# Two norms' affine moved into the MLPs, score bias by DMA, and low weight halves on VectorE through the attentions

## The chip, the cores and the metric

The kernel runs on one core of one Trainium2 chip. A core has TensorE (PE), VectorE (DVE), ScalarE (ACT), GpSimd (POOL) and SyncE (SP), each with its own in-order queue, and DMA queues beside them. The metric is the device time of one execution in microseconds; before, it is 1722.39 us, the median of three runs (1721.23 to 1723.97).

## The reference

Two layers of a diffusion transformer of width 1024 run over 512 latent tokens and 128 prompt tokens. Each layer is an attention mixer and a squared-ReLU MLP, each with a modulated input, a gated residual and a layer norm behind it. Layer 0 has differential attention, layer 1 attention over a two-dimensional neighbourhood with a learned bias.

```python
def layer_norm(x, g, b): return (x - mean(x)) * rsqrt(var(x) + eps) * g + b
def modulate(x, shift, scale): return x * (1 + scale) + shift
def sq_relu_mlp(h, w1, w2): return square(relu(h @ w1)) @ w2

for i in range(DEPTH):                         # DEPTH = 2; the same for xp (prompt) and xs (latent)
    y = mixer[i](modulate(xs, ms[0], ms[1]), caches[i], params[i])
    xs = layer_norm(ALPHA * xs + ms[2] * y, ln_g[i, 0], ln_b[i, 0])
    y = sq_relu_mlp(modulate(xs, ms[3], ms[4]), w_mlp1[i], w_mlp2[i])
    xs = layer_norm(ALPHA * xs + ms[5] * y, ln_g[i, 1], ln_b[i, 1])

# layer 1, latent tokens: window scores get a bias, context scores none
ln = einsum('bchd,bicjhd->bhcij', q, k_window) * scale + bias   # bias = rpb[rel. row, rel. col]
p = softmax(concat([ln, q @ ck * scale]))
```

## The kernel before

**Tokens and precision.** The 640 tokens are five tiles of 128 (`NTT`); the activations that a product reads are kept transposed, 1024 features by 640 tokens, as a high part and a low part (`hhi`, `hlo`, or `uhi`, `ulo` inside the MLP). Weights are split in the same way, and each product is three matmuls (`mm3`, L117 to L121): high by high, high by low, low by high.

**Weights.** They stream through a ring of five groups of 128x1024 (`RING`). For each group `conv` (L188 to L199) has ScalarE copy the raw tile to its high part `wh` (L194), and two subtractions of 128x512, the "halves", make the low part `wl` (L196). `self.pool_lo` says how many of the two GpSimd makes; the others are VectorE's. The conversion of a group is issued when an old group has been used for the last time (`used`, `done`), so conversions come in bursts of three or four at the end of a chunk. `pool_lo` is 2 at the start, 1 in most of the attentions and in the MLPs, and 2 from the steps named "X" near the end of each attention, through its projection, up to the MLP.

**Order.** TensorE's order is written by hand: the strings `ORDER0`, `ORDER1` and `ORDER_LN` name steps which `Net.run` calls. On the other engines a scheduler sets the order of the queue. In the attentions, S is a score step, T its transposes, P the product with V, B the bias of a score step. Behind the last head come the projection (o, j), the gated residual (g), the transposes of the normalised rows (h), the first up-projections (f) and W, which closes.

**Norms after attention.** For each token tile `gated` multiplies the projection by the gate (`tmp`, L1167), adds it to X (L1169 or L1171), takes statistics (L1034), and `ln_pre` (L1036 to L1044) ends in one subtract-and-multiply of 128x1024 (`X`, L1044). `ln_h` transposes X (L1073), has ScalarE apply the next modulation (its coefficients `AB` are per feature), and splits the result into `hhi` and `hlo` (L127). The norm's own g and b reach X, which is the residual of the next part, by two GpSimd instructions of 128x1024 (L1084, L1085), issued by step W. Between the layers the same functions work in the order `ORDER_LN`; there the GpSimd affine is issued tile by tile, and X then goes to DRAM (`x1`).

**MLP.** `rest` runs four groups; each has two up chunks (`ff`, then `act`: Relu on ScalarE L1230, square on VectorE L1231, split into `uhi` and `ulo`) and two down passes of five token tiles (`nat`, then `add_gated_sb`, L1117 to L1121).

**Layer-1 scores.** For a pair of heads and a block of 128 queries `scores1` makes two 128x384 score tiles. `qk_rows` (L456 to L460) does a 128-row matmul for each head with the high part of Q, then for each head a matmul of 64 rows with its low part. `bias1` (L813) prepares the tile E on GpSimd from a column mask and a table of one head pair; E has six buffers, freed by the transposes (L884).

Of the kernel before, what the change touches and what calls it, by code (L numbers as in the profile page):

```python
# [18 lines left out]
P = 128  # L19
# [30 lines left out]
    g1 j02 j13 h0 g2 j03 j04 h1 j14 g3 g4 h2 f0 f2 h3 f3 h4 f1 W  # L50
# [10 lines left out]
    h4 f3 f2 W  # L61
# [4 lines left out]
class Net:  # L66
# [163 lines left out]
    def consts(self):  # L230
# [11 lines left out]
        self.sc = c.tile([P, KT, 32], F32, name="sc")  # L242
# [78 lines left out]
    def mod_affine(self, l, s, k=None):  # L321
# [6 lines left out]
        pl, ps = (l, 0) if s == 1 else (l - 1, 1)  # L328
        g = self.lnc[:, pl, ps, 0, :].unsqueeze(2).to_broadcast([P, KT, 2])
        b = self.lnc[:, pl, ps, 1, :].unsqueeze(2).to_broadcast([P, KT, 2])  # L330
# [123 lines left out]

    def qk_rows(self, out, Q, K, q, k):
        te = self.nc.tensor  # L456
        for x in range(2):
            te.matmul(out[x], Q[:, x, q], k(K[:, x]), start=True, stop=False)
        for x, r in enumerate(HALF):
            te.matmul(out[x], Q[r, 2, q], k(K[r, x]), start=False, stop=True)  # L460

# [215 lines left out]
    def layer0_attn(self, acc0):  # L677
        nc, a = self.nc, self.a
        with self.tc.tile_pool(name="at0", bufs=1) as pool:
            self.q0 = pool.tile([P, 4, NT], F32R, name="q0")  # L680
            self.Vs, self.QKs = {}, {}
            self.pool_lo = 1
# [45 lines left out]
            def swap():  # L728
                self.pool_lo = 2
# [8 lines left out]

            def ln():
                t = pool.tile([P, 2, D], F32, tag="aTh", name="lnt")  # L740
                for x, n in enumerate(("lng", "lnb")):
                    nc.gpsimd.dma_start(t[:, x, :], a[n][0, 0].partition_broadcast(P))
                return t[:, 0, :], t[:, 1, :]
# [47 lines left out]
    def qk1(self, pool, i, x, n, c):  # L791
        nc, h, (w, hf) = self.nc, self.h, divmod(x, 2)
        if i not in self.QKs:
            Q = pool.tile([P, 3, NT], F32R, tag="Q", name=self.nm("Q"), bufs=2)
            K = pool.tile([P, 2, 768], F32R, tag="K", name=self.nm("K"), bufs=2)
            self.QKs[i] = (Q, K)
            self.cached_k(pool, self.a["ck1T"][i], K[:, :, 256:384])
# [9 lines left out]
        if w == 0:  # L807
            for s, d, k in (((0, 448, 64), (64, 0, 256)), ((0, 256, 192), (192, 512, 128)))[hf]:
                c, src = slice(d, d + k), m[:, s : s + k]
                nc.scalar.activation(Q[:, 0:2, c], src.unsqueeze(1).to_broadcast([P, 2, k]), AF.Copy, scale=-0.125)  # L810
# [609 lines left out]
```

## Time and profile before

| | |
|---|---|
| median of three runs | 1722.39 us |
| the profiled execution | 1720.29 us, its span 1718.5 us |
| mean granted TensorE clock | 0.98 |
| TensorE busy | 1630.8 us |
| VectorE busy | 1130.0 us |
| ScalarE busy | 662.0 us |
| GpSimd busy | 594.6 us |

The stages by the trace: start 0 to 54 us; layer-0 attention 54 to 405; its projection and norm to 458; first MLP to 870; norm between the layers to 930; layer-1 attention to 1224; its projection and norm to 1280; second MLP to the end. Times of instructions and waits are those of the profiled execution. A granted clock of 1.00 is the higher of TensorE's two levels, 2.4 GHz; a stretch with a lower figure ran in part at the lower one. An engine's idle time matters only where the engine that sets the end waits for it.

### The profile page before, as it was taken

Reading aid. Unit: us, or ns where it says so; the run is one execution under the profiler, and the core shown is the slowest. Engines: PE = TensorE matmul, PEld = TensorE weight load, DVE = VectorE, ACT = ScalarE, POOL = GpSimd, SP = SyncE. Lnnn points to the kernel's source line nnn. Section 1 sums busy time; section 2 is a strip of 40 time slices with the busy share of each in tenths; the row PEclk is TensorE's granted clock in tenths of the full one; section 3 lists DMA queues with packets and bytes.
Section 4 is the critical chain, followed back from the end, with each engine's and each line's share of the span. In section 5 each row is a group of like instructions: output and inputs, shape, how many; then the busy total and the mean of one; then the engine's idle time right before and its main releaser. Section 6 shows DMA issues by size and latency. Waiting matters only on the chain.

```text
span 1718.5 us, 25925 instructions
## 1 busy us (share of the span) xinstructions
PE 1630.8 (95%) x10026; PEld 1461.4 (85%) x10026; DVE 1130.0 (66%) x2015; ACT 662.0 (39%) x1338; POOL 594.6 (35%) x457
## 2 busy tenths in 40 slices
PE   8999999898799999999998999999789999999997
PEld 5798998786798988988978889997689898898996
DVE  4788778865748789798466677778684333242338
ACT  2466545643521221312234556565263122131321
POOL 2111112124632246264257233433373223324322
PEclk9999999999899999999999999999999999999999
DMA  8442234332334445353323222233133121222221
GB/s 331 134 136 95 88 126 137 108 128 67 123 99 142 165 137 184 124 184 120 99 69 128 79 79 79 78 102 115 59 109 98 50 98 62 86 64 85 85 64 62
DMA packets 59086, 187.96 MB, mean 109 GB/s; under 512 B 7396, under 2 KB 14034, under 8 KB 57938
## 3 DMA queue, kind: packets, MB, share of 16 engines
q1 hardware_dynamic: 55890, 174.89, 30.8%
q0 software_dynamic: 3072, 11.40, 1.9%
q8 instruction: 79, 1.29, 0.3%
q14 instruction: 45, 0.37, 0.1%
HBM read 176.25 MB, written 7.40 MB: 107 GB/s over the span
## 4 chain that ended last, share of the span: by engine, by line
PE 72%; DVE 15%; issue 4%; POOL 4%; ACT 3%; DMA 2%; SPq 0%; DVEq 0%; POOLq 0%; ACTq 0%
PE M L119 14%; PE M L121 14%; PE M L120 14%; PE S L121 8%; PE S L119 7%; PE S L120 7%; DVE wl L196 4%; POOL wl L196 2%; DVE hlo L127 1%; DVE X L1044 1%; POOL X L1084 1%; PE M L259 1%; PE M L595 1%; PE M L884 1%; POOL X L1085 1%
## 5 line engine op out<-in xcount | busy, mean ns | idle before, releaser
L196 POOL TENSOR_TENSOR wl<-rw,wh 128x512 fp32r<-128x512 f32 x209 | 345.7, 1674 | 589.5 <-ACT wh L194 543.5
L194 ACT CAST wh<-rw 128x1024 fp32r<-128x1024 f32 x192 | 196.9, 1050 | 347.3 <-PE M L121 270.0
L121 PE MATMUL S<-hhi,wl 128*128 128x320 f32 (+1 forms) x944 | 293.7, 311 | 6.1 <-DVE wl L196 4.7
L119 PE MATMUL S<-hhi,wh 128*128 128x320 f32 (+1 forms) x944 | 292.8, 310 | 0.0
L120 PE MATMUL S<-hlo,wh 128*128 128x320 f32 (+1 forms) x944 | 292.1, 309 | 0.0
L119 PE MATMUL M<-wh,uhi 128*128 128x512 f32 x640 | 249.6, 390 | 1.0 <-ACT uhi L126 1.0
L121 PE MATMUL M<-wh,ulo 128*128 128x512 f32 x640 | 249.3, 389 | 0.3
L120 PE MATMUL M<-wl,uhi 128*128 128x512 f32 x640 | 249.2, 389 | 0.0
L196 DVE TENSOR_TENSOR wl<-rw,wh 128x512 fp32r<-128x512 f32 x175 | 208.8, 1213 | 52.2 <-ACT wh L194 50.9
L119 PE MATMUL M<-wh,hhi 128*128 128x256 f32 (+1 forms) x640 | 202.4, 316 | 9.4 <-DVE tmp L1167 8.4
L121 PE MATMUL M<-wh,hlo 128*128 128x256 f32 (+1 forms) x640 | 197.1, 308 | 4.0 <-DVE hlo L127 3.9
L120 PE MATMUL M<-wl,hhi 128*128 128x256 f32 (+1 forms) x640 | 196.9, 308 | 2.5 <-DVE wl L196 2.5
L121 PEld LDWEIGHTS S<-hhi,wl 128*128 128x128 f32 x944 | 179.1, 190 | 10.1 <-DVE wl L196 8.3
L120 PEld LDWEIGHTS S<-hlo,wh 128*128 128x128 f32 x944 | 179.3, 190 | 0.2
L119 PEld LDWEIGHTS S<-hhi,wh 128*128 128x128 f32 x944 | 179.3, 190 | 0.2
L293 DVE SCALAR_TENSOR_TENSOR jk<-wm,cb 128x1024 bf16<-128x1024 f32 x96 | 142.5, 1484 | 1.5
L119 PEld LDWEIGHTS M<-wh,uhi 128*128 128x128 f32 x640 | 120.1, 188 | 26.5 <-ACT uhi L126 1.9
L121 PEld LDWEIGHTS M<-wh,ulo 128*128 128x128 f32 x640 | 120.1, 188 | 26.2 <-DVE ulo L127 1.1
L120 PEld LDWEIGHTS M<-wl,uhi 128*128 128x128 f32 x640 | 120.1, 188 | 24.5
L119 PEld LDWEIGHTS M<-wh,hhi 128*128 128x128 f32 x640 | 124.9, 195 | 18.0 <-DVE tmp L1167 8.9
L1231 DVE SCALAR_TENSOR_TENSOR r<-S,r 128x640 f32<-128x640 f32 (+1 forms) x62 | 48.5, 782 | 138.0 <-ACT r L1230 137.9
L121 PEld LDWEIGHTS M<-wh,hlo 128*128 128x128 f32 x640 | 124.5, 195 | 12.3 <-DVE hlo L127 7.7
(280 smaller groups left out, 3059.2 us busy)
## 6 DMA issues: line engine op xcount, KB each, us to landing
rw<-in_w SPq DMA_DIRECT2D x192, 512.0 KB, 4.1
wm<-in_wmodT SPq DMA_DIRECT2D x48, 512.0 KB, 3.5
rw<-in_wmod SPq DMA_DIRECT2D x32, 512.0 KB, 4.5
wm<-in_wmod SPq DMA_DIRECT2D x8, 1024.0 KB, 10.2
gate<-gates POOLq DMA_DIRECT2D x6, 512.0 KB, 5.0
X<-in_xT SPq DMA_DIRECT2D x8, 320.0 KB, 10.4
X<-in_xn SPq DMA_DIRECT2D x5, 512.0 KB, 5.4
x<-X SPq DMA_DIRECT2D x5, 512.0 KB, 2.8
```

The costliest lines, as they stand in the source:

```text
L119: te.matmul(out, sh, mh, start=start, stop=False)
L120: te.matmul(out, sh, ml, start=False, stop=False)
L121: te.matmul(out, sl, mh, start=False, stop=stop)
L127: nc.vector.tensor_tensor(lo, src, hi, ALU.subtract)
L194: keep(nc.scalar.copy(hi, r))
L196: keep(eng.tensor_tensor(lo[:, k], r[:, k], hi[:, k], ALU.subtract))
L259: self.nc.tensor.matmul(acc[32 * j : 32 * j + 32, :256], self.sc[:, 4 * r + j, :], w[:, j, :], start=r == 0, stop=r == 1, tile_position=(0 ...
L293: op = nc.vector.scalar_tensor_tensor(jk, ws[t], 1.0, cb[:, x, :], ALU.mult, ALU.mult, accum_out=mc[:, t, x : x + 1])
L595: nc.tensor.transpose(t[:, P * (j - j0) : P * (j - j0) + P], E[:, P * j : P * j + P], self.idf)
L884: nc.tensor.transpose(t[:, P * y : P * y + P], pr["E", b][:, x, c : c + P], self.idf)
L1044: nc.vector.tensor_scalar(x, x, mv[:, 0:1], rs, ALU.subtract, ALU.mult)
L1231: nc.vector.scalar_tensor_tensor(rv, src, 0.0, rv, ALU.max, ALU.mult)
```

## The change

It has five parts.

- *Norm affine.* The norms after the attentions no longer apply g and b at step W, which goes. In `rest`, behind the first Relu of the second up chunk of group 0, ten GpSimd instructions (`affine`: multiply, add for each tile) do it; they read `lng` and `lnb` loaded a little earlier, and the second norm's pair is loaded after them.
- *Norm between the layers.* `ln_mid` takes the place of `ln_pre` there: two scalar_tensor_tensor instructions on VectorE, (x - mean) * g and x * rstd + b, and the store of X to `x1`. `mod_affine` no longer folds g and b into those coefficients.
- *Low halves.* `pool_lo` is 0 from the layer-0 attention up to the first down pass of the first MLP, and again from the last down pass of the first MLP to the first down pass of the second: both halves on VectorE. In between it is 1, as before.
- *Scores.* Q has four slots, its low part written for both heads like its high part; `qk` does full 128-row matmuls for both, so that the low part of Q now meets the low part of K too. The swap DMA of Q doubles from 160 to 320 KB.
- *Bias.* E is loaded ready-made, 128x768 in float32, by one DMA on GpSimd's queue for each of the 32 score steps; the mask, the head-pair tables and GpSimd's work on them go. The exponential's sign conventions follow.

```diff
@@ consts, layer0_attn, layer1_attn
-        self.sc = c.tile([P, KT, 32], F32, name="sc")
+        self.sc = pool.tile([P, KT, 32], F32, name="sc")
-            self.pool_lo = 1
+            self.pool_lo = 0
             def swap():
-                self.pool_lo = 2
             def early():
-                self.pool_lo = 2
-            self.pool_lo = 1
@@ mod_affine
-        pl, ps = (l, 0) if s == 1 else (l - 1, 1)
+        if s == 0:
+            nc.vector.tensor_scalar(AB[:, 0], sc, 1.0, None, ALU.add)
+            nc.vector.tensor_copy(AB[:, 1], sh)
+            return
@@ qk1
-            Q = pool.tile([P, 3, NT], F32R, tag="Q", name=self.nm("Q"), bufs=2)
+            Q = pool.tile([P, 4, NT], F32R, tag="Q", name=self.nm("Q"), bufs=2)
-                nc.vector.scalar_tensor_tensor(Q[:, 2, c], src, -0.125, Q[:, 0, c], ALU.mult, ALU.subtract)
+                nc.vector.scalar_tensor_tensor(Q[:, 2:4, c], two, 0.125, Q[:, 0:2, c], ALU.mult, ALU.subtract)
-                    nc.sync.dma_start(Q[HALF[1 - y], y, :].bitcast(F32), Q[r, y, :].bitcast(F32))
+                    nc.sync.dma_start(Q[HALF[1 - y], y::2, :].bitcast(F32), Q[r, y::2, :].bitcast(F32))
@@ bias1
-        zero = (256, 128, 0, 128)[b]
-        nc.gpsimd.memset(E[:, :, zero : zero + P], 0.0)
...
-            nc.gpsimd.tensor_tensor(
-                E[:, :, d : d + n], mk[:, m : m + n].unsqueeze(1).to_broadcast([P, 2, n]), T[:, :, s : s + n], ALU.subtract
-            )
+        self.nc.gpsimd.dma_start(E, self.a["bias"][i, b])
@@ scores1, ctx_scores1
-        self.qk_rows(out, Q, K, qs, kv)
+        self.qk(out, Q, K, qs, kv)
@@ new, behind ln_pre
+    def ln_mid(self, st, X, t, g, b, dst):
+        nc, x, sml = self.nc, X[:, t, :], self.sml
+        mv = sml.tile([P, 2], F32, name=self.nm("mv"), tag="mv", bufs=2)
+        rs = sml.tile([P, 1], F32, name=self.nm("rstd"), tag="rstd", bufs=2)
+        nc.vector.bn_aggr(mv, st[:, t, :, :])
+        nc.scalar.activation(rs, mv[:, 1:2], AF.Sqrt, bias=self.eps)
+        nc.vector.scalar_tensor_tensor(x, x, mv[:, 0:1], g, ALU.subtract, ALU.mult)
+        nc.vector.reciprocal(rs, rs)
+        nc.vector.scalar_tensor_tensor(x, x, rs, b, ALU.mult, ALU.add)
+        nc.sync.dma_start(dst, x)
+
+    def affine(self, X, t, g, b, after):
+        nc, x = self.nc, X[:, t, :]
+        op = nc.gpsimd.tensor_tensor(x, x, g, ALU.mult)
+        self.tc.add_manual_dep(
+            op.ins, after.ins.name,
+            mybir.DependencyInfo(mybir.DependencyClass.Sync, mybir.DependencyReason.DATA), reason="affine",
+        )
+        nc.gpsimd.tensor_tensor(x, x, b, ALU.add)
@@ ln_h
-        def affine():
-            nc.gpsimd.tensor_tensor(x, x, g, ALU.mult)
-            nc.gpsimd.tensor_tensor(x, x, b, ALU.add)
-            if dst is not None:
-                nc.sync.dma_start(dst, x)
@@ rest
-                        g, b = self.ln_tiles(pool, l, 1)
+                        g, b = self.ln_tiles(pool, l, 0)
-                            act(us, 4 * c + f, s2[:, :, :320])
+                            op = act(us, 4 * c + f, s2[:, :, :320])
+                            if gr == 0 and f == 0:
+                                for t in range(NTT):
+                                    self.affine(X, t, g, b, op)
+                                g, b = self.ln_tiles(pool, l, 1)
                 if gr < 3:
                     for n in range(2):
+                        self.pool_lo = 1
...
-                    self.ln_pre(st, X, t)
+                    self.ln_mid(st, X, t, g, b, self.x1[t])
...
+            self.pool_lo = 0
             for t in range(NTT):
                 down(t, 0)
```

How this moves instructions shows at three places. The first is GpSimd at the end of the layer-1 norm, before: L1084 and L1085 are the affine, `lnt` its two rows, wl the low halves.

```order
L1085 TENSOR_TENSOR X_12112<-X_12112,lnt_12459 128x1024
L196 TENSOR_TENSOR wl_12627<-rw_12249,wh_12626 128x512 x2
L196 TENSOR_TENSOR wl_12640<-rw_12262,wh_12639 128x512 x2
L196 TENSOR_TENSOR wl_12647<-rw_12618,wh_12646 128x512 x2
L1084 TENSOR_TENSOR X_12112<-X_12112,lnt_12458 128x1024
L196 TENSOR_TENSOR wl_12660<-rw_12631,wh_12659 128x512 x2
L1085 TENSOR_TENSOR X_12112<-X_12112,lnt_12459 128x1024
L1084 TENSOR_TENSOR X_12112<-X_12112,lnt_12458 128x1024
```

After the change GpSimd's queue in the second MLP reads so; L1065 are loads, L1019 and L1024 the affine, and the next half is one of the first down passes.

```order
L1065 DMA lng_12944<-in_lng 128x1024
L1065 DMA lnb_12946<-in_lnb 128x1024
L1019 TENSOR_TENSOR X_12024<-X_12024,lng_12944 128x1024 x2
L1024 TENSOR_TENSOR X_12024<-X_12024,lnb_12946 128x1024 x2
L1019 TENSOR_TENSOR X_12024<-X_12024,lng_12944 128x1024 x2
L1024 TENSOR_TENSOR X_12024<-X_12024,lnb_12946 128x1024 x2
L1019 TENSOR_TENSOR X_12024<-X_12024,lng_12944 128x1024
L1024 TENSOR_TENSOR X_12024<-X_12024,lnb_12946 128x1024
```

The affine and all ten halves have left the norm; the affine stands behind a load and a Relu of the MLP. The second place is VectorE at the end of the layer-1 norm, before, with the last token tile's gate product (L1167), addition (L1169), statistics and X (L1044).

```order
L1167 TENSOR_TENSOR tmp_12666<-M_12554,gv 128x512
L1040 BN_AGGR mv_12576<-st_12457 128x2
L127 TENSOR_TENSOR hlo<-hs_12595,hhi 128x4x128
L1169 TENSOR_TENSOR X_12112<-X_12112,tmp_12666 128x512
L1043 RECIPROCAL rstd_12578<-rstd_12578 128x1
L1167 TENSOR_TENSOR tmp_12670<-M_12606,gv 128x512
L1044 TENSOR_SCALAR X_12112<-X_12112,mv_12576,rstd_12578 128x1024
```

After, at the same place (L1136, L1138 and L1004 are those lines now):

```order
L127 TENSOR_TENSOR hlo<-hs_12502,hhi 128x4x128
L196 TENSOR_TENSOR wl_12521<-rw_12147,wh_12520 128x512
L1003 RECIPROCAL rstd_12485<-rstd_12485 128x1
L196 TENSOR_TENSOR wl_12534<-rw_12160,wh_12533 128x512
L1004 TENSOR_SCALAR X_12024<-X_12024,mv_12483,rstd_12485 128x1024
L196 TENSOR_TENSOR wl_12534<-rw_12160,wh_12533 128x512
L196 TENSOR_TENSOR wl_12547<-rw_12173,wh_12546 128x512 x2
L1136 TENSOR_TENSOR tmp_12573<-M_12461,gv 128x512
L1136 TENSOR_TENSOR tmp_12577<-M_12513,gv 128x512
L196 TENSOR_TENSOR wl_12554<-rw_12525,wh_12553 128x512 x2
L1138 TENSOR_TENSOR X_12024<-X_12024,tmp_12573 128x512
```

The ten halves that GpSimd had now stand in VectorE's queue, six of them ahead of the last tile's gate products. The third place is VectorE at the first down pass of the first MLP, before; r is the square of the last up-projection, `ulo` its low part, L1117 the first down product.

```order
L196 TENSOR_TENSOR wl_5633<-rw_5397,wh_5632 128x512
L196 TENSOR_TENSOR wl_5646<-rw_5410,wh_5645 128x512
L196 TENSOR_TENSOR wl_5659<-rw_5423,wh_5658 128x512
L1231 SCALAR_TENSOR_TENSOR r_5678<-S_5601,r_5678 128x640
L127 TENSOR_TENSOR ulo_5261<-r_5678,uhi_5260 128x640
L196 TENSOR_TENSOR wl_5672<-rw_5637,wh_5671 128x512
L1117 TENSOR_TENSOR tmp_5708<-M_5683,gate_932_5430 128x512
```

And after:

```order
L196 TENSOR_TENSOR wl_5634<-rw_5384,wh_5633 128x512 x2
L196 TENSOR_TENSOR wl_5647<-rw_5397,wh_5646 128x512 x2
L196 TENSOR_TENSOR wl_5660<-rw_5410,wh_5659 128x512 x2
L1195 SCALAR_TENSOR_TENSOR r_5679<-S_5602,r_5679 128x640
L127 TENSOR_TENSOR ulo_5248<-r_5679,uhi_5247 128x640
L196 TENSOR_TENSOR wl_5673<-rw_5638,wh_5672 128x512 x2
L1087 TENSOR_TENSOR tmp_5709<-M_5684,gate_932_5417 128x512
```

Six halves instead of three stand ahead of the last square.

## Rows read from the trace of the kernel before

**Rows 1.** The page's first part: busy us, share of the span, instructions.
```profile
PE 1630.8 (95%) x10026; PEld 1461.4 (85%) x10026; DVE 1130.0 (66%) x2015; ACT 662.0 (39%) x1338; POOL 594.6 (35%) x457
```

**Rows 2.** Table by stretch: us, busy per engine, granted clock, DMA share, GB/s.
```profile
54.00:405.00 351.00, 335.93 (x2491) 302.33 (x2492) 269.34 (x694) 195.06 (x488) 55.91 (x55) 0.98 0.35 118
...
405.00:458.00 53.00, 38.17 (x206) 32.23 (x206) 47.76 (x58) 25.08 (x59) 39.62 (x19) 0.87 0.16 50
...
510.00:540.00 30.00, 30.00 (x134) 24.82 (x134) 22.90 (x32) 4.22 (x4) 7.01 (x4) 1.00 0.44 139
870.00:930.00 60.00, 53.30 (x287) 45.77 (x286) 50.26 (x53) 29.79 (x64) 43.04 (x22) 0.94 0.31 107
...
930.00:1224.00 294.00, 285.26 (x1909) 258.18 (x1908) 202.68 (x498) 159.99 (x376) 105.89 (x145) 0.99 0.29 93
1224.00:1280.00 56.00, 43.05 (x249) 37.63 (x248) 49.50 (x55) 25.78 (x60) 42.93 (x20) 0.91 0.15 48
```

**Rows 3.** Waits of TensorE: for whom, us in total, times, longest.
```profile
PE M L1073 <- DVE X L1044: 17.9, 9, 6.6
PE M L119 <- DVE tmp L1167: 8.4, 1, 8.4
PE S L121 <- DVE wl L196: 4.7, 8, 0.8
```

**Rows 4.** Timeline of VectorE in the layer-1 norm: start, us, instruction.
```profile
1247.93 0.80 DVE L1044 TENSOR_SCALAR X<-X,mv,rstd 128x1024 f32<-128x1024 f32 x1
...
1249.85 0.68 DVE L127 TENSOR_TENSOR hlo<-hs,hhi 128x512 fp32r<-128x512 f32 x1
...
1260.70 14.67 DVE L127 TENSOR_TENSOR hlo<-hs,hhi 128x512 fp32r<-128x512 f32 x6
```

**Rows 5.** VectorE by line and form, 1224 to 1280 us: busy us, mean ns.
```profile
L127 DVE TENSOR_TENSOR hlo<-hs,hhi 128x512 fp32r<-128x512 f32 x10 | 19.1, 1944 | 0.0
```

**Rows 6.** Timeline of GpSimd in the layer-1 norm.
```profile
1266.39 2.85 POOL L1085 TENSOR_TENSOR X<-X,lnt 128x1024 f32<-128x1024 f32 x1
...
1277.69 2.40 POOL L1085 TENSOR_TENSOR X<-X,lnt 128x1024 f32<-128x1024 f32 x1
```

**Rows 7.** Low halves: VectorE's by the page, GpSimd's in 1224 to 1280 us.
```profile
L196 DVE TENSOR_TENSOR wl<-rw,wh 128x512 fp32r<-128x512 f32 x175 | 208.8, 1213 | 52.2 <-ACT wh L194 50.9
...
L196 POOL TENSOR_TENSOR wl<-rw,wh 128x512 fp32r<-128x512 f32 x10 | 16.2, 1642 | 3.4 <-ACT wh L194 3.4
```

**Rows 8.** Timeline of VectorE at the first down pass of the first MLP.
```profile
501.26 0.69 DVE L196 TENSOR_TENSOR wl<-rw,wh 128x512 fp32r<-128x512 f32 x1 [2.09 <-ACT wh L194]
502.20 3.15 DVE L196 TENSOR_TENSOR wl<-rw,wh 128x512 fp32r<-128x512 f32 x2 [0.25 <-ACT wh L194]
...
515.21 1.22 DVE L293 SCALAR_TENSOR_TENSOR jk<-wm,cb 128x1024 bf16<-128x1024 f32 x1
```

**Rows 9.** TensorE by line and form, 930 to 1224 us: the scores.
```profile
L458 PE MATMUL S<-K,Q 128*128 128x384 f32 x64 | 17.1, 348 | 0.8 <-DVE mn L864 0.8
L460 PE MATMUL S<-K,Q 64*128 64x384 f32 x64 | 14.1, 438 | 0.0
```

**Rows 10.** Waits of all engines: GpSimd's for a free bias tile.
```profile
POOL E L832 <- PE M L884: 45.6, 6, 12.3
```

**Rows 11.** Timelines of TensorE and VectorE at one score step.
```profile
1050.29 1.06 PE L884 MATMUL M<-idf,E 128*128 128x128 f32 x8
...
1053.50 0.55 DVE L864 CUSTOM_DVE_ANT_0 E<-S,E 128x384 f32<-128x384 f32 x1
```

**Rows 12.** DMA issues of the page: count, KB each, median us to landing.
```profile
X<-rnd POOLq DMA_DIRECT2D x6, 320.0 KB, 3.6
...
lnb<-in_lnb POOLq DMA_DIRECT2D x2, 512.0 KB, 8.3
```

**Rows 13.** Timeline of ScalarE in the first MLP: the Relu named in the change.
```profile
481.90 0.70 ACT L1230 ACTIVATE r<-S 128x640 f32<-128x640 f32 x1 [2.56 <-PE S L121]
```

**Rows 14.** Timeline of TensorE: the first down-projection of the first MLP.
```profile
502.76 0.39 PE L119 MATMUL M<-wh,uhi 128*128 128x512 f32 x1
```

More of the change, by code (lines that the diff above doesn't have):

```diff
@@ L453, in qk @@
             te.matmul(out[x], Q[:, 2 + x, q], k(K[:, x]), start=False, stop=True)
[L455 to L460, printed above, removed]
     def v_evac(self, pool, i, t, src, cache, out):
@@ L737, in swap @@
                 late["X"] = self.x_tile(a["xn"])
[L739 to L743, printed above, removed]
             op = self.op
@@ L992, in swap @@
                     fn()
-            def ln():
-                ts = [pool.tile([P, D], F32, tag="PT", name=self.nm("lnt"), bufs=3) for _ in range(2)]
-                for t, n in zip(ts, ("lng", "lnb")):
-                    nc.gpsimd.dma_start(t, a[n][1, 0].partition_broadcast(P))
-                return ts
             op = self.op
@@ L1081, in ln_h @@
             self.split(h[0][:, ks, cs], h[1][:, ks, cs], hs)
-        def affine():
-            nc.gpsimd.tensor_tensor(x, x, g, ALU.mult)
-            nc.gpsimd.tensor_tensor(x, x, b, ALU.add)
-            if dst is not None:
-                nc.sync.dma_start(dst, x)
-        if now:
-            affine()
-        return affine
     def rows_bc(self, pool, tag, src):
@@ L1121, in add_gated_sb, with proj_ops @@
             eng.tensor_tensor(X[:, t, cs], X[:, t, cs], tmp, ALU.add)
-    def proj_ops(self, pool, l, late, early, free, ready, tag, ln):
+    def proj_ops(self, pool, l, late, early, free, ready, tag):
         nc, n, op = self.nc, NCH * l + 6, self.op
         seq = [(hf, t) for hf in range(2) for t in range(NTT)]
-        accs, ms, sb, fs, first, tail = {}, {}, [], [], {}, []
+        accs, ms, sb, fs, first = {}, {}, [], [], {}
         box = {}
@@ L1175, in norm @@
         def norm(t):
-            tail.append(self.ln_h(pool, late["X"], t, *box["gb"], self.AB[l][1], None, (tag[2], tag[1]), False))
+            self.ln_h(pool, late["X"], t, self.AB[l][1], (tag[2], tag[1]))
         def up(f):
@@ L1187, in up @@
             self.ff(NCH * l + 8, f, 0, CUT, fs[f])
-        def close():
-            for fn in tail:
-                fn()
         for x, (hf, t) in enumerate(seq):
@@ L1359, in layout, with inside @@
     jj = np.arange(32)[None, :]
-    def mask(c, k):
+    def inside(c, k):
         c0 = np.clip(c - 8, 0, 48)
-        m = np.where((k >= c0) & (k < c0 + 16), 0.0, BIG).astype(np.float32)
-        m = np.broadcast_to(m[:, None, :, None], (16, 8, m.shape[1], 8))
-        return m.reshape(P, -1)
-    masks = np.concatenate([mask(qi, jj[:, :24]), mask(16 + qi, 8 + jj), mask(48 + qi, 40 + jj[:, :24])], 1)
+        m = (k >= c0) & (k < c0 + 16)
+        return np.broadcast_to(m[:, None, :, None], (16, 8, m.shape[1], 8)).reshape(1, P, -1)
+    left, mid, right = inside(qi, jj[:, :24]), inside(16 + qi, 8 + jj), inside(48 + qi, 40 + jj[:, :24])
+    win = win.reshape(16, P, 256)
+    bias = np.full((4, 16, P, 384), -BIG, np.float32)
+    for b, zero, parts in (
+        (0, 256, ((64, 64, left),)),
+        (1, 128, ((0, 0, mid[:, :, :128]), (256, 128, mid[:, :, 128:]))),
+        (2, 0, ((128, 0, mid),)),
+        (3, 128, ((256, 0, right[:, :, :128]), (0, 128, right[:, :, 128:]))),
+    ):
+        bias[b, :, :, zero : zero + P] = 0.0
+        for d, o, m in parts:
+            n = m.shape[2]
+            bias[b, :, :, d : d + n] = np.where(m, win[:, :, o : o + n], np.float32(-BIG))
     out = dict(
@@ L1387, in layout @@
         cv1=g["cache_l1_v"][0].reshape(P, D),
-        rpb=win.reshape(8, 2, P, 256).transpose(0, 2, 1, 3),
-        mask=masks,
+        bias=bias.reshape(4, 8, 2, P, 384).transpose(1, 0, 3, 2, 4),
     )
```

56 lines of the change are left out of this document (19 added, 37 removed).

## Prediction

> **What bounds the kernel now.** First the busy shares: TensorE 95%, VectorE (DVE) 66%, GpSimd (POOL) 35% [rows 1]. Nothing but TensorE can be the bound over the whole span, so an edit gains only where TensorE is not running. The table by stretch shows where that is [rows 2]. In the MLP, at 510 to 540 us, it is busy 30.00 of 30 us at granted clock 1.00: nothing to gain. In the projection and norm of layer 0 (405 to 458) it is busy 38.17 of 53 us at clock 0.87. Idle time is 14.8 us; the low clock costs about 0.13 x 38.2 = 5.0, together 19.8 us lost. In the same way 870 to 930 (norm after the first MLP) loses 6.7 + 3.2 = 9.9, and 1224 to 1280 (projection and norm of layer 1) 13.0 + 3.9 = 16.9. The long attention stretches lose 15.1 + 6.7 = 21.8 (54 to 405) and 8.7 + 2.9 = 11.6 (930 to 1224), thinly spread. These five sums, 80 us, are what the change can reach.
>
> Next, who TensorE waits for [rows 3]: its transposes (L1073) wait 17.9 us for the normalised X of DVE, 6.6 at worst; one projection matmul waits 8.4 us for DVE's tmp, and up-projections wait 4.7 us for low parts wl. All of these are DVE. Is DVE slow because it has much to do? The timeline says no. With GpSimd idle a 128x1024 X takes 0.80 us and a 128x512 hlo 0.68 [rows 4]; but in 1224 to 1280 ten hlo took 19.1 us, 1944 ns each [rows 5]. Six hlo in a row from 1260.70 take 14.67 us [rows 4], 2.45 each, exactly while GpSimd runs its 2.85 us affine instructions back to back [rows 6]. One hlo gets through for each GpSimd instruction: on these operands, all in SBUF, the two engines alternate. The weight halves show the same: 1213 ns mean on DVE over the whole run and 1642 on GpSimd in this stretch [rows 7], against 0.69 for one on DVE alone [rows 8].
>
> **The change part by part.** Sums are made against the profiled execution, 1720.3 us, which lies 2.1 under the median of the runs.
>
> (a) Norm of layer 1. GpSimd was busy 42.93 of 56 us [rows 2]; all of that leaves the stretch (ten affine instructions, ten weight halves). DVE gains on the hlo alone 19.1 - 10 x 0.68 = 12.3 us; taking the X, add and STT instructions at their shortest I estimate some 21 in all. It gets ten halves more, 10 x 0.68 = 6.8. So its 49.5 us become about 35, less than TensorE's own 39 or so at full clock. Of TensorE's 16.9 us lost I take 11 as gained; the rest is the first tile's chain (projection end, tmp, add, stats, X, transpose), which only latency sets, and which now has eight halves queued ahead of the last tile's tmp. Bounds: 6 (the halves land on that chain) and 14.
>
> (b) Norm of layer 0. The same edit: POOL's 39.62 us go, nine halves (6.1 us) come. Of 19.8 lost I take 10; here the queue puts halves ahead of the rescaling of the last heads, 1 to 2 us late. Bounds 5 and 13.
>
> (c) Norm between the layers. GpSimd's 43.04 us go. But each tile's one X of 0.80 us becomes two scalar_tensor_tensor over 128x1024. The nearest row is jk, the same form and size, 1.22 us [rows 8] (with a narrower output), so 2.44 - 0.80 = 1.6 more per tile, 8.2 in all, and eight halves come, 5.4. Against an estimated 21 us of DVE freed, 7 are left. The multiply by g needs no rstd and can stand beside the Sqrt, but the second instruction stands ahead of the transposes. Gain 5 of 9.9; bounds 1 and 8.
>
> (d) Up-projections of the first group no longer wait for halves that alternate, and the layer-1 projections no longer wait for GpSimd's: 4 of the 4.7 us in [rows 3]; bounds 2 and 5.
>
> (e) Full-row scores. A 64-row matmul took 438 ns, a 128-row one 348, 64 each [rows 9]. If the difference is real occupancy, 64 x 0.09 = 5.8; the pairs' columns stay the same. I take 5; bounds 0 and 6. The low part of Q is written for both heads and its swap DMA doubled: eight pairs x 640 more columns, about 0.85 us each by the hlo's rate, 7 us of DVE within 294, inside (g).
>
> (f) Layer-0 attention. By the order 103 halves change engine; the row of GpSimd's halves [rows 7] reads x10 in (a)'s stretch, and the same row x9 and x8 in those of (b) and (c), x28 here and x30 in (g)'s. A pair done in turns takes about 1.3 + 0.68, on DVE alone 1.36: a burst ends earlier, but all of it is now ahead of DVE's evacuations. Gain 2; bounds +3 and -6.
>
> (g) Layer-1 attention. Of GpSimd's 105.89 us here [rows 2] the halves and the bias tables go; what DVE instructions waited beside them comes back. Added are 30 x 0.68 + 7 = 27 us, which take DVE from 203 towards 230 of 294: still no bound. Of the 11.6 us lost I take 4 as gained; bounds +2 and -8.
>
> (h) Bias tables. GpSimd's memsets waited for a free buffer in only 6 steps, 45.6 us in all [rows 10]; elsewhere buffers are free early and a load is hidden. In a tight step the buffer's transposes start at 1050.29 and last 1.06, and DVE reads the next table at 1053.50 [rows 11], 2.2 us later. The nearest load, 320 KB by the same queue, lands in 3.6 us [rows 12], a bit more for 393 KB: 2 us late. Three such steps, partly covered by projections: +2. Bounds 0 and +15 (by the row of 8.3 us, six steps).
>
> (i) The affine in the MLP. Ten instructions that need 2.40 us undisturbed [rows 6] now start behind the Relu that ends at 481.90 + 0.70 = 482.6 [rows 13]. TensorE reaches the first down-projection at 502.76 [rows 14]. By 501.3, when DVE takes the first half for it [rows 8], 18.7 us have passed, of which three ulo of 640 columns took 2.5 (0.85 each by the hlo's rate): 6.7 of the ten are done. From there one half gets through per affine: halves 1, 2, 3, 4 end near 502.6, 505.7, 508.8 and 511.9, 5 and 6 at 512.5 and 513.1; then r, uhi, ulo to 515.4. Before, a half needed 1.6 here (3.15 for two, [rows 8]). TensorE wants them 0.69 us per k-tile: half 2 at 505.1 (late 0.6), half 3 at 506.4 (2.4 more), half 4 (2.4 more), the last ulo at 508.0 + 5.4 (2.0 more): 7.4 us, in a place that lost nothing [rows 2]. I take 7 for each layer, +14. Bounds +8 and +18.
>
> Start, the wait for the modulation vectors, and the final norm are unchanged: 0.
>
> Sum: -11 - 10 - 5 - 4 - 5 - 2 - 4 + 2 + 14 = -25. 1720.3 - 25 = 1695.3, plus 2.1: **1697 us**.
>
> **A rule that speaks against (h).** The trace shows the gpsimd-issued load of 320 KB landing in 3.6 us and one of 512 KB in 8.3 [rows 12], so a slow case exists. The Trainium skill, page "SBUF — State Buffer", section "SBUF: two separate sides", says that a DMA issued from GpSimd has its descriptors written by that engine, which cannot do so while a VectorE instruction in a two-port mode holds the ports that both share; the transfer then looks blocked. By that rule a DVE made busier delays the tables (rival 2); the 3.6 us row, taken beside a DVE busy 269 of 351 us, does not show it.
>
> **The rivals.**
> 1. The affine is hidden. If r and ulo do not hold GpSimd up and it gets ahead, 7.8 of ten are done by 501.3 and the stall halves, and the norms give their upper bounds: -25 - 7 - 8 = 1682. For: TensorE keeps 20 us from Relu to first use. Against: 24 us do not fit into 20.
> 2. Bias tables late. Loads of about 8 us instead of 3.6: six steps some 2 to 4 us later each, +15: 1712. For: [rows 12], second row. Against: that row is the last of four loads issued together and a broadcast.
> 3. Slower: DVE's queue becomes the bound in the attentions. A burst of eight halves is 5.5 us in which no evacuation passes, where four on DVE took 4 x 1.2 = 4.9 and let the other four go by. If instead each of the 58 moved halves of both attentions lands with its 0.68 on TensorE's path, that is +39, without the -6 of (f) and (g): 1742. It decides from about two thirds of them (+26). For: DVE is busy 269 of 351 us in layer 0 [rows 2]. Against: TensorE lost only 21.8 us there, with the other half of each group already on DVE and slowed.
>
> **How the numbers follow.** Forecast (1688 to 1707) 0.55; rival 1 (under 1688) 0.17; rival 2 or a part of rival 3 (1707 to 1719) 0.16; no change within 0.2%, which is about what a measurement of this kernel can tell, 0.05; rival 3 in full 0.07. Faster 0.88. The range 1680 to 1714 leaves out about 0.08 below and 0.12 above.
>
> **What would show it.** Right: hlo near 0.68 us and X near 0.8 in both attention norms, each of these stretches some 10 us shorter and at a granted clock over 0.95; no GpSimd in it; scores at one length. For (i): TensorE waiting on wl and ulo for 5 to 9 us some 20 us after the first 128x640 Relu of each MLP, beside GpSimd's ten instructions. For (c): the two new instructions at 1.2 us each; if they take 2 us the gain there is gone. Rival 2: DVE's score reduction waits for E's DMA. Rival 3: evacuations behind wl in both attentions. The forecast is wrong if DVE still needs over 45 us in the norms without GpSimd beside it.

## Result and the profile after

The changed kernel takes 1700.77 us (median of four runs, 1697.76 to 1702.16) against 1721.81 (the four runs of the kernel before; the 1722.39 above is the median of the first three): a ratio of 0.9874, 95% interval 0.9857 to 0.9891. The forecast was 1697, the range 1680 to 1714. The page's first part (columns as in [rows 1]):

```profile
PE 1620.8 (95%) x10026; PEld 1466.2 (86%) x10026; DVE 1116.3 (66%) x2121; ACT 662.4 (39%) x1338; POOL 370.3 (22%) x280
```

VectorE does 103 halves more, and is still busy for 14 us less than before; GpSimd lost 224 us of work. The norms as stretches (layer 0, between the layers, layer 1), followed by the first down passes of the two MLPs. The first and third stretch hold about the work of those of [rows 2] (218 and 247 matmuls against 206 and 249); the second ends a little earlier in the work (257 against 287):

```profile
401.00:446.00 45.00, 38.21 (x218) 32.86 (x217) 36.92 (x68) 25.65 (x61) 0.00 (x0) 0.92 0.19 59
862.00:915.00 53.00, 48.92 (x257) 42.35 (x256) 42.00 (x65) 29.13 (x63) 2.59 (x2) 0.94 0.38 135
1206.00:1254.00 48.00, 41.57 (x247) 36.71 (x247) 40.18 (x75) 29.32 (x70) 2.10 (x4) 0.96 0.28 94
486.00:502.00 16.00, 12.63 (x49) 9.90 (x48) 14.86 (x13) 5.22 (x6) 9.85 (x6) 0.79 0.48 145
1289.00:1305.00 16.00, 11.87 (x50) 8.91 (x50) 14.91 (x12) 5.22 (x6) 10.21 (x6) 0.85 0.42 131
```

The norms became shorter, with GpSimd (the last busy figure of a row, ahead of the granted clock) nearly gone. The last two rows show a loss: TensorE is busy 12.63 and 11.87 of 16 us, at granted clocks of 0.79 and 0.85. Before, it was busy without a break at these places, at 1.00. VectorE in the layer-1 norm, by line and form (busy us, mean ns; idle time before):

```profile
L127 DVE TENSOR_TENSOR hlo<-hs,hhi 128x512 fp32r<-128x512 f32 x10 | 6.8, 679 | 3.7 <-ACT hhi L126 3.7
...
L196 DVE TENSOR_TENSOR wl<-rw,wh 128x512 fp32r<-128x512 f32 x10 | 6.5, 679 | 0.2 <-ACT wh L194 0.2
```

The ten hlo that took 1944 ns each [rows 5] take 679 once GpSimd is out of the stretch, and so do the ten added halves.

**Where the time went.** Both kernels issue 10026 matmuls in nearly the same order, so the start of the same matmul can be compared between the two traces (us; negative is earlier in the changed kernel; the last column is worked out from the two starts):

| stage (time before) | shift at its start, at its end | change |
|---|---|---|
| start, 0 to 60 | 0, -1.1 | -1.1 |
| layer-0 attention, 60 to 400 | -1.1, -3.0 | -1.9 |
| its norm, 400 to 460 | -3.0, -13.2 | -10.2 |
| first up-projections, 460 to 500 | -13.2, -14.1 | -0.9 |
| first down pass, 500 to 540 | -14.1, -7.0 | **+7.1** |
| norm between the layers, 880 to 946 | -6.9, -10.7 | -3.8 |
| first layer-1 projections, 946 to 960 | -10.7, -13.1 | -2.4 |
| layer-1 attention, 960 to 1220 | -13.1, -18.3 | -5.2 |
| its norm, 1220 to 1280 | -18.3, -26.0 | -7.7 |
| second up-projections, 1280 to 1300 | -26.0, -28.0 | -2.0 |
| second down pass, 1300 to 1340 | -28.0, -20.2 | **+7.8** |

The rest of both MLPs moves by 0.1 us. Two places give back 15 of 35 us. Each column rests on one trace, and traces differ a little also where kernels are alike: in the layer-0 attention e7 and e9 below lose 1.6 us against the changed kernel, whose work they do there, and e5 2.0 against the kernel before, whose work it does there. A change of 1 to 2 us in a long stage is thus not shown by one trace.

### The profile page after: what moved, and what is told of

It reads as the page before. It is cut to its first block, busy times and chain, and to the rows that moved or that the text cites. A ratio compares the mean times of both kernels' runs of the same rounds, so it can differ in the third digit from the quotient of the medians.

```text
span 1699.3 us, 25833 instructions
## 1 busy us (share of the span) xinstructions
PE 1620.8 (95%) x10026; PEld 1466.2 (86%) x10026; DVE 1116.3 (66%) x2121; ACT 662.4 (39%) x1338; POOL 370.3 (22%) x280
## 5 line engine op out<-in xcount | busy, mean ns | idle before, releaser
L196 DVE TENSOR_TENSOR wl<-rw,wh 128x512 fp32r<-128x512 f32 x278 | 247.9, 931 | 51.6 <-ACT wh L194 50.0
L196 POOL TENSOR_TENSOR wl<-rw,wh 128x512 fp32r<-128x512 f32 x106 | 182.2, 1738 | 405.7 <-ACT wh L194 404.1
## 6 DMA issues: line engine op xcount, KB each, us to landing
wm<-in_wmod SPq DMA_DIRECT2D x8, 1024.0 KB, 10.7
```

The costliest lines, as they stand in the source:

```text
L196: keep(eng.tensor_tensor(lo[:, k], r[:, k], hi[:, k], ALU.subtract))
```

## The experiments

**The affine in the MLP.** Timeline of VectorE, then of GpSimd, of the changed kernel at the first down pass (start, us, instruction):

```profile
484.25 2.80 DVE L127 TENSOR_TENSOR ulo<-r,uhi 128x640 fp32r<-128x640 f32 x1 [0.79 <-ACT uhi L126]
487.17 10.05 DVE L196 TENSOR_TENSOR wl<-rw,wh 128x512 fp32r<-128x512 f32 x6
497.14 0.81 DVE L1195 SCALAR_TENSOR_TENSOR r<-S,r 128x640 f32<-128x640 f32 x1
```
```profile
483.96 5.36 POOL L1024 TENSOR_TENSOR X<-X,lnb 128x1024 f32<-128x1024 f32 x2
489.27 2.82 POOL L1019 TENSOR_TENSOR X<-X,lng 128x1024 f32<-128x1024 f32 x1
492.18 2.69 POOL L1024 TENSOR_TENSOR X<-X,lnb 128x1024 f32<-128x1024 f32 x1
```

Six halves take 10.05 us. Until the affine ends, at 494.87, one half gets through for each affine instruction, in turns of 2.7 to 2.9 us; this holds three of the six, and the last three take 0.68 us each. To see whether the turns cause the loss, one kernel leaves the affine out (e1) and one places memsets of a like total length there (e8):

```diff
                             if gr == 0 and f == 0:
-                                for t in range(NTT):
-                                    self.affine(X, t, g, b, op)
                                 g, b = self.ln_tiles(pool, l, 1)
```

> The changed kernel without the ten affine instructions in both MLPs (their multiply by g and add of b is left out; the loads stay). Theory: the 7.1 us and 7.8 us that TensorE loses at the first down pass of each MLP come from VectorE's halves taking turns with these instructions, so about 15 us go: 1700.8 - 15 = 1686, and the six halves in VectorE's queue there take 6 x 0.69 = 4.1 us in place of 10.05. Rival: the six halves ahead of the last square are late by themselves, as all six are now VectorE's; then at least half of the loss stays and the time is 1693 or more.

```diff
                             if gr == 0 and f == 0:
-                                for t in range(NTT):
-                                    self.affine(X, t, g, b, op)
+                                for t in range(2 * NTT):
+                                    for z in (g, b):
+                                        ms = nc.gpsimd.memset(z, 0.0)   # waits for the Relu, as affine does
...
```

> The changed kernel with the ten affine instructions of each MLP replaced by twenty memsets of 128x1024 behind the same Relu (the norm's multiply and add are left out, and the loaded rows are overwritten). GpSimd is busy for a time like that of the affine, but reads no operand. Theory: the turns are tied to instructions that read operands in SBUF, so VectorE's six halves take 0.69 us each and the time is that without the affine, 1686. Rival: any GpSimd instruction makes VectorE wait: 1696 or more.

Without the affine: 1686.52 us, ratio 0.9794 (0.9779 to 0.9809). With memsets: 1686.42, 0.9790 (0.9772 to 0.9808). Timelines of VectorE without the affine, and of VectorE and GpSimd with the memsets:

```profile
486.06 3.70 DVE L196 TENSOR_TENSOR wl<-rw,wh 128x512 fp32r<-128x512 f32 x6 [2.09 <-ACT wh L194]
```
```profile
485.20 0.83 DVE L127 TENSOR_TENSOR ulo<-r,uhi 128x640 fp32r<-128x640 f32 x1 [0.79 <-ACT uhi L126]
488.12 3.70 DVE L196 TENSOR_TENSOR wl<-rw,wh 128x512 fp32r<-128x512 f32 x6 [2.09 <-ACT wh L194]
```
```profile
484.72 1.00 POOL L1229 MEMSET lnb<- 128x1024 f32 x1
485.61 1.00 POOL L1229 MEMSET lng<- 128x1024 f32 x1
486.50 1.01 POOL L1229 MEMSET lnb<- 128x1024 f32 x1
```

The six halves take 3.70 us, and the 15 us are back (7.1 and 7.8 us by the starts, at the two first down passes): the affine causes them, and the greater number of halves by itself costs nothing. For the memsets the halves say nothing, since GpSimd had finished at 487.5, just before them; the ulo does: it keeps its 0.83 us with memsets on both sides, where it took 2.80 us beside the affine. So on these rows a GpSimd instruction that reads no operand doesn't hold VectorE up.

The cure keeps the work and places it where VectorE has little to do (e2):

```diff
...
-                            op = act(us, 4 * c + f, s2[:, :, :320])
-                            if gr == 0 and f == 0:
-                                for t in range(NTT):
-                                    self.affine(X, t, g, b, op)
-                                g, b = self.ln_tiles(pool, l, 1)
+                            op, low = act(us, 4 * c + f, s2[:, :, :320])
+                            if gr == 0 and f in (0, 3):
+                                for t in range(3) if f == 0 else range(3, NTT):
+                                    self.affine(X, t, g, b, op if f == 0 else low)
+                                if f == 3:
+                                    g, b = self.ln_tiles(pool, l, 1)
```

> The changed kernel with the affine of token tiles 0 to 2 behind the Relu as now (six instructions, 6 x 2.4 + three turns with ulo = 17 us, done before the halves at 18.6 us after the Relu) and of tiles 3 and 4 behind the last ulo. Theory: it gains the same 15 us as leaving the affine out, 1686, since tile 3 is needed only some 16 us into the down pass. Rival: the four instructions that come later collide with the next halves or hold up the gate products, and give back 3 us or more for each layer: 1692 or more.

It takes 1688.06 us, 0.9805 (0.9786 to 0.9823): better than both kernels. GpSimd, then VectorE at the down pass:

```profile
484.21 2.41 POOL L1024 TENSOR_TENSOR X<-X,lnb 128x1024 f32<-128x1024 f32 x1
495.86 5.73 POOL L1019 TENSOR_TENSOR X<-X,lng 128x1024 f32<-128x1024 f32 x2 [9.24 <-DVE ulo L127]
```
```profile
489.66 3.70 DVE L196 TENSOR_TENSOR wl<-rw,wh 128x512 fp32r<-128x512 f32 x6 [2.09 <-ACT wh L194]
...
495.85 3.49 DVE L196 TENSOR_TENSOR wl<-rw,wh 128x512 fp32r<-128x512 f32 x2
```

The six urgent halves are free of turns. The next two are not (3.49 us), but those belong to a group that is wanted later. By the starts it gets back 5.7 us of the 7.1 in layer 0 and all 7.8 in layer 1.

**Which engine makes the halves.** The prediction priced the affine's leaving and the halves' move as two terms that add. One kernel is the change with the halves as before (e5), one is the kernel before with only the halves moved (e6):

```diff
-            self.pool_lo = 0      # e5, from the changed kernel: layer 0 and layer 1
+            self.pool_lo = 1
...
             def swap():           # and in early()
+                self.pool_lo = 2
...
```
```diff
-            self.pool_lo = 1      # e6, from the kernel before: layer 0 and layer 1
+            self.pool_lo = 0
...
             def swap():           # and in early()
-                self.pool_lo = 2
...
```

> The changed kernel with only the low halves shared out as before (GpSimd makes one of two in the attentions and MLPs, both from step X to the MLP). Theory of the prediction: the affine alone explains about 27 of GpSimd's 43 us in a norm, so the norms keep a little over half of their 18 us, the up-projections and attentions lose their 6 to 10, and the first down pass stays late since GpSimd's halves queue behind the affine: 1708 to 1716. Rival: which engine makes a half does not matter once the affine is out of the norms: 1701, within 3 us.

> The kernel before with only the low halves moved to VectorE in the same stretches as in the change; the affine stays in the norms. Theory of the prediction: each moved half takes away a turn of GpSimd's of 1.3 us or more and adds 0.68 us on VectorE, so the norms gain some 8 to 10 us together, the up-projections 4, the attentions a few: 1705 to 1712. Rival: VectorE's queue is the bound in the attentions and the halves land on the path: 1722 or more.

The first takes 1711.46 us, 0.9940 (0.9923 to 0.9957), within what was expected, but not by the theory stated: the norms did not keep a little over half of their 18 us, they kept all of it (-11.7 and -6.9 us in the two attention norms). The second missed by 19 us: 1731.25, 1.0054 (1.0037 to 1.0070), *slower* than before. The time is that of the rival, its place is not: the shift against the kernel before grows by only 0.5 and 1.3 us in the two attentions, but by 7.3 us in 440 to 460 and by 7.7 in 1250 to 1280, so it loses in the norms. VectorE and GpSimd there, in layer 0:

```profile
450.90 2.22 DVE L1040 TENSOR_SCALAR X<-X,mv,rstd 128x1024 f32<-128x1024 f32 x1
453.04 5.66 DVE L127 TENSOR_TENSOR hlo<-hs,hhi 128x512 fp32r<-128x512 f32 x2
```
```profile
450.16 2.41 POOL L1080 TENSOR_TENSOR X<-X,lnt 128x1024 f32<-128x1024 f32 x1 [8.67 <-PE M L1069]
452.65 2.72 POOL L1081 TENSOR_TENSOR X<-X,lnt 128x1024 f32<-128x1024 f32 x1
455.31 2.83 POOL L1080 TENSOR_TENSOR X<-X,lnt 128x1024 f32<-128x1024 f32 x1
```

In layer 1, first GpSimd and VectorE before, then VectorE in this kernel, at the last tile's additions to X:

```profile
1250.85 9.36 POOL L196 TENSOR_TENSOR wl<-rw,wh 128x512 fp32r<-128x512 f32 x6 [3.39 <-ACT wh L194]
```
```profile
1252.60 1.78 DVE L1169 TENSOR_TENSOR X<-X,tmp 128x512 f32<-128x512 f32 x1
...
1256.65 1.16 DVE L1171 SCALAR_TENSOR_TENSOR X<-X,tmp 128x512 f32<-128x512 f32 x1
```
```profile
1268.50 2.88 DVE L1165 TENSOR_TENSOR X<-X,tmp 128x512 f32<-128x512 f32 x1
1271.31 2.83 DVE L1167 SCALAR_TENSOR_TENSOR X<-X,tmp 128x512 f32<-128x512 f32 x1
```

Before, GpSimd's halves, 1.56 us each, stood between its affine instructions, and these additions took 1.78 and 1.16 us beside them. With no halves of its own left GpSimd has nothing between them, so VectorE meets one of 2.4 to 2.9 us at each turn, right in the chain to the last transposes. Eight moved halves stand ahead of these additions too; how much each of the two costs was not tried apart.

With the affine gone the same move gains 10.7 us, but not in the norms: without it they gain 11.7 and 6.9 us, with it 10.2 and 7.7. So what the norms gain is the affine's. What the changed kernel is ahead of e5 is spread: by the starts 3.9 us in the layer-0 attention (of which up to 2 can be the difference between traces), 3.5 in the first layer-1 projections and the attention behind them, 3.0 at the first down passes, where in e5 GpSimd's halves queue behind the affine (waits of TensorE):

```profile
PE M L120 <- POOL wl L196: 12.3, 2, 6.2
```

**The norm between the layers** (e7), undone alone:

```diff
-                    self.ln_mid(st, X, t, g, b, self.x1[t])
+                    self.ln_pre(st, X, t)
...                       # and g, b back in mod_affine
+                    nc.gpsimd.tensor_tensor(X[:, t, :], X[:, t, :], g, ALU.mult)   # after ln_h
+                    nc.gpsimd.tensor_tensor(X[:, t, :], X[:, t, :], b, ALU.add)
```

> The changed kernel with the norm between the layers as before: one subtract-and-multiply on VectorE, the affine on GpSimd behind each tile, g and b folded into the modulation; the halves there stay on VectorE. Theory of the prediction: the change is worth 5 us there, part of it from the halves, so taking it back costs 2 to 5 us: 1703 to 1706. Rival: the two longer instructions ahead of the last transposes (a wait of 4.1 us in the changed kernel) cost as much as GpSimd's turns did: 1700 or less.

1709.27 us, 0.9926 (0.9909 to 0.9942): 8.5 us more than the changed kernel, beyond both theories. The starts put it in two places. About 4 us are lost in the norm (870 to 915 us), as in e6: the halves stay on VectorE beside GpSimd's affine, and five of them take 7.42 us, where they take 3.10 in the changed kernel. Another 5.1 us are lost behind it, in 930 to 945: ScalarE waits for a load of cached values, `in_cv`, and TensorE then 2.4 us for a high weight part behind it on ScalarE's queue. VectorE, then ScalarE's wait:

```profile
901.74 7.42 DVE L196 TENSOR_TENSOR wl<-rw,wh 128x512 fp32r<-128x512 f32 x5
```
```profile
ACT V L126 <- DMA X<-in_cv: 6.2, 1, 6.2
```

With the affine back in this norm the last X is stored later, and that load, which stands behind the store in SyncE's queue, is issued at 923.94 in place of 912.35 us, just behind four bias loads instead of 3.9 us ahead of the first one; it lands after 6.30 us instead of 2.12 (see the bias tables, e4). So `ln_mid` also keeps the bias loads out of the way of this one, and these two edits don't add either.

Against the kernel before, the changed one gained 3.8 us in this norm. Its two new instructions, in 862 to 915 us, and the wait that they leave:

```profile
L1012 DVE SCALAR_TENSOR_TENSOR X<-X,mv,lng 128x1024 f32<-128x1024 f32 x5 | 6.4, 1283 | 0.1
L1014 DVE SCALAR_TENSOR_TENSOR X<-X,rstd,lnb 128x1024 f32<-128x1024 f32 x5 | 6.4, 1280 | 0.1
```
```profile
PE M L1053 <- DVE X L1014: 4.1, 1, 4.1
```

**Scores** (e3):

```diff
+        for x, r in enumerate(HALF):
+            te.matmul(out[x], Q[r, 2 + x, q], k(K[r, x]), start=False, stop=True)
-            te.matmul(out[x], Q[:, 2 + x, q], k(K[:, x]), start=False, stop=True)
```

> The changed kernel with the low part of Q multiplied in 64 rows again, head by head, everything else as changed. Theory: 64 rows cost 0.09 us more for each 128x384 matmul, so 5 us come back in 930 to 1220: 1706. Rival: TensorE had slack there or only the latency differs and not the occupancy: 1701, within 1.5 us.

1707.42 us, 0.9913 (0.9895 to 0.9931): 6.6 us more, 5.5 of them by the starts in the layer-1 attention (960 to 1200 us of the changed kernel). The low-part matmul in that kernel, then in the changed one (by line and form, mean ns behind the busy us):

```profile
L463 PE MATMUL S<-K,Q 64*128 64x384 f32 x64 | 14.4, 446 | 0.0
```
```profile
L456 PE MATMUL S<-K,Q 128*128 128x384 f32 x64 | 21.6, 337 | 0.0
```

The mean length is not where the time goes. The 64 short-row matmuls keep TensorE busy for 14.4 us and not 64 x 446 ns, because two of them run at once. One score step of the kernel before, with the matmul that follows it:

```profile
1045.45 0.52 PE L458 MATMUL S<-K,Q 128*128 128x384 f32 x2
1045.89 0.44 PE L460 MATMUL S<-K,Q 64*128 64x384 f32 x2
1046.27 0.42 PE L119 MATMUL M<-hhi,wh 128*128 128x320 f32 x1
```

The two of 64 rows start 3 ns apart. What costs is the change to 64 rows and back: they start 0.27 us after the matmul ahead of them and hold the next one back for 0.37, where full rows follow each other every 0.175 us. A step of four takes 0.82 us before and in e3, 0.71 in the changed kernel (medians); over the 32 steps and the 8 of the context that is 31.0 against 26.6 us, 4.4 us.

**Bias tables.** The load alone, put into the kernel before (e4), and 26 of the 32 loads replaced in the changed kernel (e9):

```diff
-        nc.gpsimd.memset(E[:, :, zero : zero + P], 0.0)      # e4, from the kernel before
...
+        self.nc.gpsimd.dma_start(E, self.a["bias"][i, b])
```
```diff
-        self.nc.gpsimd.dma_start(E, self.a["bias"][i, b])    # e9, but for the first six
+        self.nc.gpsimd.memset(E, 0.0)
```

> The kernel before with the bias tables loaded by DMA on GpSimd's queue and nothing else changed (the signs of Q and of the exponential follow). Theory of the prediction: +2 us, as three tight score steps get their table late: 1724. Rival: GpSimd is relieved of 54 us of memsets and subtractions which took turns with VectorE, and that gains more than the late tables cost: 1718 or less.

> The changed kernel with 26 of its 32 bias tables replaced by a memset of E on GpSimd (those biases and masks are left out), at the same place in GpSimd's queue, so the table is there about 1 us after the buffer is free and 10 MB of loads go. Theory of the prediction: the late tables cost the changed kernel 2 us: 1699. Rival, from the 6 us that the load alone cost the kernel before: the loads cost 5 us or more here too, in part by delaying weight loads: 1696 or less.

The first takes 1727.63 us, 1.0032 (1.0023 to 1.0042), some 5.5 us more than before. Most of it is one event, 4.7 us by the starts: at the start of layer 1 four bias loads are issued within 1.7 us, just ahead of a 128 KB load of cached values on SyncE's queue, which lands after 7.28 us (3.47 before). ScalarE waits for it, and behind it on ScalarE's queue a high weight part (waits of ScalarE, then of TensorE):

```profile
ACT V L126 <- DMA X<-in_cv: 7.0, 1, 7.0
```
```profile
PE M L119 <- ACT wh L194: 3.7, 1, 3.7
```

The changed kernel doesn't have that wait: its load of cached values is issued 3.9 us ahead of the first bias load and lands after 2.12 us. There the bias loads land in 5.4 us, the median, and VectorE's score reduction waited three times, 2.0 us in all:

```profile
E<-in_bias POOLq DMA_DIRECT2D x32, 384.0 KB, 5.4
```
```profile
  DMA E<-in_bias: 2.0, 3
```

Without them it takes 1698.36 us, 0.9858 (0.9838 to 0.9879), an interval that overlaps the changed kernel's; the shift against it within 960 to 1220 is only -0.7 us. So the tables cost 1 to 2 us, as forecast, and not 5, as long as the first of them (kept in e9) stay out of the way of the cached values.

**What is left in the layer-1 norm** (e10):

```diff
+            if self.pool_lo == 3:
+                nc.gpsimd.memset(lo[:, k].bitcast(F32), 0.0)
+                continue
...
             def early():
+                self.pool_lo = 3
...
```

> The changed kernel with the low halves between step X and the MLP of layer 1 written as zeros by GpSimd memsets (those low parts are left out), so ten halves of 0.68 us leave VectorE's queue in the layer-1 norm and GpSimd still takes no turns. Theory: what is left of that norm's loss is VectorE's own work, since the changed kernel's VectorE has no idle time there from 1212 to 1239; then 3 to 6 us go: 1695 to 1698. Theory of the prediction: the rest is the latency of the first tile's chain, which the halves do not lengthen: 1700, within 1.5 us.

1696.20 us, 0.9842 (0.9826 to 0.9858). Of the 4.6 us, 1.3 stand in the trace's first 20 us, which the edit doesn't touch; 3.3 are from the norm (2.0, in 1210 to 1254 us) and from one place ahead of it (1.3, at 1187, where six halves precede the scaling of a score tile). Waits of TensorE, the changed kernel in 1200 to 1254 us, then this one in 1200 to 1250:

```profile
PE M L119 <- DVE tmp L1136: 3.2, 1, 3.2
PE M L1053 <- DVE X L1004: 2.0, 2, 1.4
PE M L1053 <- DVE tmp L1136: 1.2, 1, 1.2
```
```profile
PE M L119 <- DVE tmp L1141: 3.2, 1, 3.2
PE M L1058 <- ACT wh L194: 1.6, 1, 1.6
```

The waits on the last tiles' X and on tmp, 3.2 us, are the halves' doing; in their place comes one of 1.6 us for a high weight part, which is why the norm itself gets only 2.0 us shorter. The 3.2 us for an earlier tmp, ahead of which no halves stand, remain. Both theories hold for a part.

If VectorE bounds what is left, ScalarE could take its subtract-and-multiply (e11, on top of e2):

```diff
-        nc.vector.tensor_scalar(x, x, mv[:, 0:1], rs, ALU.subtract, ALU.mult)
...
+        nc.vector.tensor_scalar(nm, mv[:, 0:1], rs, -1.0, ALU.mult, ALU.mult)
+        nc.scalar.activation(x, x, AF.Identity, bias=nm, scale=rs)
```

> The kernel with the split affine, and the subtract-and-multiply of 128x1024 of both attention norms moved from VectorE (0.80 us) to ScalarE (some 1.05 us by its copies of that size), with one more 128x1 instruction on VectorE. Theory: VectorE's own work bounds these norms now, so 5 x 0.65 us leave its queue in each and 2 to 5 us go from both together: 1683 to 1686. Rival: ScalarE's copies of raw weights and its modulation stand ahead of it and the chain to the last transposes gets longer: 1688 or more.

No gain: 1691.77 us, 0.9820 (0.9802 to 0.9839), an interval that overlaps e2's, and the time of the rival. The transposes now wait for ScalarE:

```profile
PE M L1055 <- ACT X L1006: 5.1, 4, 2.6
```

## Why the prediction was right, and by how much its steps were off

The sum was -25; the starts of the last matmul differ by 20.1 us, the profiled executions by 19.2 and the medians by 21.0. By its steps:

- **(i), the affine in the MLP, +14: right, +14.9.** It named the place, the six halves, and that they pass one for each affine instruction. Within the loss its split was off: it held four halves back and made all of the loss waiting, 7.4 us, of them 2.0 for the last ulo. Three were held back, and in layer 0 TensorE waited twice, both times for wl. In 486 to 502 us TensorE was idle for 16 - 12.63 = 3.4 us, and the clock that fell with the stalls cost about 0.21 x 12.63 = 2.7 (granted 0.79): behind the second wait matmuls of the same form take 0.63 us instead of 0.39, up to 501.6:

```profile
495.47 0.80 PE L120 MATMUL M<-wl,uhi 128*128 128x512 f32 x1 [1.80 <-DVE wl L196]
496.06 0.63 PE L121 MATMUL M<-wh,ulo 128*128 128x512 f32 x1
...
502.08 0.40 PE L121 MATMUL M<-wh,ulo 128*128 128x512 f32 x1
```

- **(b), the layer-0 norm, -10: right, -10.2**, but from the affine alone: with the halves left on GpSimd (e5) it is -11.7. Its granted clock, 0.92, did not reach the 0.95 that the prediction had as a sign. **(d), -4:** -0.9 - 2.0 and most of the -2.4 of the first layer-1 projections, about -5. **(f), -2:** -1.9, no more than traces of that stage differ by, so not shown.
- **(a), the layer-1 norm: the step was mis-sized, -11 against -7.7.** It took all but the first tile's latency as gained. The halves ahead of the last tile, which it named (it counted eight ahead of the last tmp; there are six, and two more ahead of the addition to X), cost 2.0 us in that stretch (e10), most of the difference. The rest, 1.3 us, is not traced; 3.2 us of waiting for a tmp remain there without any halves.
- **(c), -5: -3.8.** The two instructions took 1.28 us each, against the 1.22 of the row used. The second one, ahead of the last transposes, leaves 4.1 us of waiting.
- **(e), (g), (h) together -7: -5.2.** Scores: 4.4 by their own steps, 5.5 in the attention by undoing them, 5 forecast. The number was right by luck: 64 x 0.09 us took each 64-row matmul as longer by itself, but these run two at a time, and the cost is at the change of form. Bias: 1 to 2, 2 forecast. So (g), -4, is the term that was too large: by subtraction 0 to -3 are left for it. Undoing the halves alone (e5) shows 1.7 us from them in 960 to 1200, no more than traces differ by, and the doubled low part of Q with its swap was not tried alone.

What carried the forecast but does not hold in general is that the terms add. In the sum each half cost 0.68 us on VectorE and gave back its turn. That fails beside the affine: e6 and e7, whose expectations rested on adding, lay 19 and 3 us above the ends of theirs, e7 in part for a second pair that does not add, the bias loads and the late load of cached values.

On the rule of the Trainium skill, page "SBUF — State Buffer", section "SBUF: two separate sides", that the descriptors of a load issued from GpSimd can't be written while a VectorE instruction in a two-port mode holds the shared ports: no run here shows it, and it is not enough for it that VectorE is busier, as the prediction had it. The bias loads did take 5.4 us, more than the 3.6 of [rows 12] for a slightly smaller one, but by the changed kernel's trace their length goes with the loads beside them: of four issued together from 968.8 us the first landed after 3.5 us and the last after 6.8, and the first of four from 1000.0 after 3.2, with VectorE busy for 3.12 of these 3.2 us. The path lost 1 to 2 us only. The same section of the Trainium skill says that a VectorE instruction with two SBUF inputs is in conflict only with a GpSimd instruction that reads SBUF; the ulo beside memsets (0.83 us) and beside the affine (2.80 us) agrees.

## What to carry to other kernels

Where VectorE and GpSimd work on SBUF operands side by side, price an instruction by what the other engine runs at that moment, not by its own length: a 0.68 us half beside a 2.7 us affine takes a turn of 2.5 to 3. Moving work off GpSimd pays if what stays on GpSimd in that stretch is short or nothing, and a long GpSimd instruction belongs where VectorE's next urgent work is further away than the whole sequence takes: ask how many of them are still to run then, and split the sequence there (12.7 us for a few lines here). Test two edits that share such a resource together and apart, since one of them alone can have the other sign. And when a mean length suggests a gain, look at the starts: two matmuls that run at once share it.

## What the runs showed that was not expected

- The same move of halves to VectorE is worth -10.7 us with the affine out of the norms (1711.46 to 1700.77) and +10.2 with it inside (1721.07 to 1731.25).
- A 128 KB load issued just behind four loads of 384 KB for data wanted later landed after 7.28 us (e4) and 6.30 (e7), and ScalarE waited 7.0 and 6.2 us for it; without them ahead it landed after 2.12 us in the changed kernel and 3.47 before.
- Memsets of 128x1024 took 0.95 to 1.01 us on GpSimd and left VectorE's two-operand instructions at their shortest; the affine's instructions of the same size took 2.4 to 2.8 us and didn't.
